# Routing of two experts: a bit search after the loop, or ranks counted in the loop

## The chip, the cores and the metric

One of the eight cores of a Trainium2 chip runs the whole program. The metric is device time in microseconds (us), from the runs and from one profiled execution. PE is TensorE, DVE is VectorE, ACT is ScalarE, POOL is GpSimd, SP is SyncE; each takes its own instructions strictly in the order in which they stand, and waits where the next one isn't ready.

## The reference

One block: a gated linear attention and a Hyena branch, an output projection with a residual, and then a mixture of 16 experts in which every expert chooses its 128 best tokens of 1,024.

```python
def _ec_moe(h, w_router, w_gate, w_up, w_down):
    cap = EC_FACTOR * L // N_EXPERTS            # 128
    aff = jax.nn.softmax((h @ w_router).astype(jnp.float32), axis=-1)
    vals, idx = lax.top_k(jnp.swapaxes(aff, 1, 2), cap)
    xs = h[bidx, idx]
    hid = jax.nn.silu(jnp.einsum('becd,edf->becf', xs, w_gate)) * jnp.einsum('becd,edf->becf', xs, w_up)
    y = jnp.einsum('becf,efd->becd', hid, w_down) * vals[..., None].astype(h.dtype)
    return jnp.zeros_like(h).at[bidx, idx].add(y.astype(h.dtype))
```

## The kernel before, in words

Tokens lie in 8 tiles of 128 (NT). The last loop ahead of the experts runs over the tiles from 7 down to 0, in three steps that are offset by one turn each: `gla_out(i)` makes the attention output, `residual(i)` multiplies by `w_out` (the `pout` matmuls), adds the residual and writes rows to `d_acc` and `d_h`, and `router(i)` computes the affinities of the tile's 128 tokens to the 16 experts: `aff[:, :, i]`, a token on each partition.

After the loop stands the routing. `select(e0, ne, tag, bits)` finds the 128 best tokens for `ne` experts at once by a search over the bits of a float: in each round DVE makes a set of thresholds (`thr`) and compares all affinities with them (`ge`), PE counts over the tokens by 8 matmuls with a matrix of ones (`psel`), and DVE keeps the highest threshold that at least 128 tokens reach (L1283, L1284). A round can't begin before the one ahead is done. `select(0, 2, "a", 5)` serves experts 0 and 1 in 6 rounds of five bits; `select(2, 14, "b", 2)` serves experts 2 to 15 in 15 rounds of two bits. Afterwards `gt`, `eq`, `need`, `keep` and two prefix sums on PE turn the threshold into `pos`, the place of each chosen token from 1 to 128.

`route(e)` compares `pos` with the numbers 1 to 128 (`oh`, L1320, 128x1024 on DVE), gets the token numbers by 8 matmuls (`pi`), writes them to `ix`, and POOL gathers the rows `xs` from `d_h` by an indirect DMA. `transposed` turns them (`ptx`) and splits them in a high and a low part (`thi`, `tlo`).

An expert reads three weights of 8 tiles (128x1024) each: gate, up, down. For a tile ACT makes the high part (`ehi`) and DVE the low part (`elo`), with 5 and 4 buffers, and PE runs 6 matmuls (`pex`, L150 to L152). So a weight is 48 `pex` matmuls. In order of work expert 0 goes gate(0), up(0), gate(1), down(0); inside up(0), after its third tile, the code asks for the transposed rows of expert 1 and for `route(2)`, and inside gate(1) for the transposed product `sg` that down(0) needs. `route(2)` needs all of `select` "b".

The code is written in this order, but a scheduler that lays the program out at build time decides where each instruction stands on its engine, and on the chip that order is fixed. SP issues the weight loads (L1222) into 21 buffers for gate and up and 8 for down, and each load waits for its buffer.

Of the kernel before, what the change touches and what calls it, by code (L numbers as in the profile page):

```python
# [10 lines left out]
F32 = mybir.dt.float32  # L11
F32R = mybir.dt.float32r
BF16 = mybir.dt.bfloat16
I32 = mybir.dt.int32
# [28 lines left out]
def shape_constants():  # L43
    f = np.float32
    out = {}
    quarter = D // 4
    omega = (1.0 / (f(10000.0) ** (np.arange(quarter, dtype=f) / f(quarter)))).astype(f)
    er = (np.arange(16, dtype=f)[:, None] * omega).astype(f)
    ec = (np.arange(64, dtype=f)[:, None] * omega).astype(f)
    out["posr"] = np.concatenate([np.sin(er), np.cos(er)], -1).astype(f)  # L50
    pc = np.concatenate([np.sin(ec), np.cos(ec)], -1).astype(f)
    out["posc"] = np.concatenate([pc, pc], 0)
    out["pos"] = np.concatenate([np.repeat(out["posr"], 64, 0), np.tile(out["posc"], (8, 1))], 1).reshape(8, 128, 1024)
    out["ident"] = np.eye(P, dtype=f)

    n1 = np.arange(8)[None, :, None]
    n2 = np.arange(128)[:, None, None]
    k2 = np.arange(128)[None, None, :]
    th = 2 * np.pi * (k2 + 0.5) * (n1 + 8 * n2) / 2048.0
    fc, fs = np.cos(th), -np.sin(th)  # L60
    out["fmat"] = np.stack([fc, fs], 1).astype(f)
    out["fneg"] = (-fs).astype(f)
    out["imat"] = np.stack([fc.transpose(2, 1, 0) / 1024.0, fs.transpose(2, 1, 0) / 1024.0], 1).astype(f)

    t = np.linspace(0.0, 1.0, L, dtype=f)[:, None]
    w = (f(2.0 * math.pi) * np.arange(L, dtype=f)[:, None] / f(L)).astype(f)
    bands = np.linspace(1e-4, 15, 16, dtype=f)[None, :]
    fw = (bands * w).astype(f)
    z = np.concatenate([t, np.cos(fw), -np.sin(fw)], -1).astype(f)
    n = (np.arange(8)[:, None] + 8 * np.arange(128)[None, :]).reshape(-1)  # L70
    out["zfeat"] = z[n].T.astype(f)
    deltas = np.abs(np.linspace(math.log(1e-2) / 1.5, math.log(1e-2) / 0.3, HYW, dtype=f))
    dec = np.exp(-t * deltas).astype(f)[n].reshape(8, 128, 4, 128)
    out["decay"] = dec.transpose(2, 1, 0, 3).astype(f)

    i16 = 1.0 / 16.0
    tok, col = np.meshgrid(np.arange(P), np.arange(2 * (CH + 2)), indexing="ij")
    pre = (tok // CH == col // (CH + 2)) & (tok % CH < col % (CH + 2))
    out["pre"] = (pre * i16).astype(f)
    ss, cc = np.meshgrid(np.arange(P) % CH, np.arange(CH), indexing="ij")  # L80
    out["smask"] = np.stack([ss <= cc, ss >= cc], 1).astype(np.int32)
    ss, cc = np.meshgrid(np.arange(P), np.arange(P), indexing="ij")
    out["before"] = (ss < cc).astype(f)
    out["slot"] = np.broadcast_to(np.arange(1, P + 1, dtype=f), (P, P)).copy()
    out["sel"] = np.tile(np.eye(32, E, dtype=f), (4, 1))
    tid = np.zeros((P, NT, 2), f)
    tid[:, :, 0] = np.arange(P)[:, None]
    tid[:, :, 1] = P * np.arange(NT)[None, :]
    out["tokid"] = tid
    for b in (5, 2):  # L90
        dig = np.zeros((P, 30 // b, 1 << b), np.int32)
        for i in range(30 // b):
            dig[:, i, :] = np.arange(1 << b) << (30 - b * (i + 1))
        out[f"digit{b}"] = dig
    return {"c_" + k: np.ascontiguousarray(v) for k, v in out.items()}
# [3 lines left out]
def tile_gla_hyena_moe(ctx: ExitStack, tc: tile.TileContext, io: dict, out: bass.AP):  # L99
# [22 lines left out]
    def s2(shape, dt=F32, name="s2"):  # L122
        return s2p.tile(shape, dt, name=name, tag="s2")
# [10 lines left out]
    def cload(name, shape, dt=F32, pool=None, src=None):  # L134
        t = (pool or const).tile(shape, dt, name=name)
        SY.dma_start(t, io["c_" + name] if src is None else src)
        return t
# [807 lines left out]
    def gb(tag, bufs):  # L945
        return lambda shape, name: psg.tile(shape, F32, name=name, tag=tag, bufs=bufs)

    ga, gc, gd, ge1 = gb("ga", 2), gb("gc", 2), gb("gd", 1), gb("ge", 1)

    def chunk_updates(i, e4, vs):  # L950
# [114 lines left out]
    SY.dma_start(slotf, io["c_slot"])  # L1065
    V.tensor_copy(slot, slotf)
    tokid = cload("tokid", [P, NT, 2], pool=keep)
    digit = {b: cload(f"digit{b}", [P, 30 // b, 1 << b], I32, pool=keep) for b in (5, 2)}
    ones = keep.tile([P, P], BF16, name="ones")
    V.memset(ones, 1.0)  # L1070
    before = keep.tile([P, P], BF16, name="before")
    befr = s2([P, P], name="befr")
    SY.dma_start(befr, io["c_before"])
    V.tensor_copy(before, befr)
    ws = [wout_tile(k, op_tile) for k in range(4)]
    p2a.close()
    g2 = p2.enter_context(tc.tile_pool(name="g2", bufs=1, side="right", reuse_waits="tile"))

    def h4(shape, name, tag, bufs, dt=F32):
        return g2.tile(shape, dt, name=name, tag=tag, bufs=bufs)  # L1080


    diag = [g2.tile([P, NH, P], F32, name=f"diag{x}") for x in range(2)]
# [98 lines left out]
        V.reciprocal(sm, sm)  # L1182
        V.tensor_scalar(aff[:, :, i], ex, sm, None, op0=ALU.mult)

    outs, rows = [], []
    for i in reversed(range(-2 - 1, NT)):
        if i >= 0:
            outs.append((i, gla_out(i)))
        if rows:
            router(*rows.pop(0))  # L1190
        if outs and (i < 0 or len(outs) > 1):
            o_ = outs.pop(0)
            rows.append((o_[0], *residual(*o_)))
    p2.close()
    st_stack.close()
    early_stack.close()
# [9 lines left out]
    def pT(shape, name):  # L1206
        return pse.tile(shape, F32, name=name, tag="t", bufs=2)
# [35 lines left out]
    def select(e0, ne, tag, bits):  # L1243

        aff_ = aff[:, e0:e0 + ne]

        def tl(shape, dt, name, bufs=1):
            return mt(shape, dt, name + tag, name + tag, bufs)

        def column_sums(ps, mask):  # L1250
            for t in range(NT):
                T.matmul(ps, ones, mask[:, :, t], start=t == 0, stop=t == NT - 1)  # L1252

        def prefix(ps, mask):
            T.matmul(ps, before, mask, start=True, stop=False)
            for s in range(1, NT):
                T.matmul(ps[:, :, s:], ones, mask[:, :, 0:NT - s], start=False, stop=s == NT - 1)

        if e0 == 0:
            def pr(n):  # L1260
                return pT([P, n], "psel")
        else:
            acc = pse.tile([P, D], F32, name="psel", tag="ex", bufs=3)
            flip = [0]

            def pr(n):
                flip[0] ^= 512
                return acc[:, flip[0]:flip[0] + n]

        base = tl([P, ne], F32, "base")  # L1270
        V.memset(base, 0.0)
        nd = 1 << bits
        for b in range(30 // bits):
            thr = tl([P, nd, ne], F32, "thr", 2)
            V.tensor_tensor(thr.bitcast(I32), digit[bits][:, b, :, None].to_broadcast([P, nd, ne]),
                            base.bitcast(I32)[:, None, :].to_broadcast([P, nd, ne]), op=ALU.bitwise_or)
            ge = tl([P, nd - 1, ne, NT], BF16, "ge")
            V.tensor_tensor(ge, aff_[:, None].to_broadcast([P, nd - 1, ne, NT]),
                            thr[:, 1:nd, :, None].to_broadcast([P, nd - 1, ne, NT]), op=ALU.is_ge)
            pc = pr((nd - 1) * ne)  # L1280
            column_sums(pc, ge.rearrange("p q e t -> p (q e) t"))
            upper = thr[:, 1:nd].rearrange("p q e -> p (q e)")
            V.scalar_tensor_tensor(upper, pc, float(CAP) - 0.5, upper, op0=ALU.is_ge, op1=ALU.mult)  # L1283
            V.tensor_reduce(base, thr.rearrange("p q e -> p e q"), AX.X, ALU.max)  # L1284
        thb = base[:, :, None].to_broadcast([P, ne, NT])
        gt = tl([P, ne, NT], BF16, "gt")
        V.tensor_tensor(gt, aff_, thb, op=ALU.is_gt)
        eq = tl([P, ne, NT], BF16, "eq")
        V.tensor_tensor(eq, aff_, thb, op=ALU.is_equal)
        pg_ = pr(ne)  # L1290
        column_sums(pg_, gt)
        need = tl([P, ne], F32, "need")
        V.tensor_scalar(need, pg_, -1.0, float(CAP), op0=ALU.mult, op1=ALU.add)
        pq_ = pr(ne * NT).rearrange("p (e t) -> p e t", t=NT)
        prefix(pq_, eq)
        keep = tl([P, ne, NT], BF16, "keep")
        V.tensor_tensor(keep, pq_, need[:, :, None].to_broadcast([P, ne, NT]), op=ALU.is_lt)
        V.tensor_mul(keep, keep, eq)
        V.tensor_add(keep, keep, gt)
        pp = pr(ne * NT).rearrange("p (e t) -> p e t", t=NT)  # L1300
        prefix(pp, keep)
        V.scalar_tensor_tensor(pos[:, e0:e0 + ne], pp, 1.0, keep, op0=ALU.add, op1=ALU.mult)

    NF = 2
    select(0, NF, "a", 5)

    tv = mp.tile([P, E, NT, 5], BF16, name="tv")
    V.tensor_copy(tv[:, :, :, 0:2], tokid[:, None].to_broadcast([P, E, NT, 2]))
# [8 lines left out]
    def route(e):  # L1317
        pi = pT([P, 5], "pi")
        oh = mt([P, NT, P], BF16, "oh", "s2", NS)
        V.tensor_tensor(oh, slot[:, None, :].to_broadcast([P, NT, P]),  # L1320
                        pos[:, e, :, None].to_broadcast([P, NT, P]), op=ALU.is_equal)
        for t in range(NT):
            T.matmul(pi, oh[:, t], tv[:, e, t], start=t == 0, stop=t == NT - 1)
        ix = tiny.tile([P, 1], I32, name="ix", bufs=4)
# [121 lines left out]
```

## Time and profile before

| | us |
|---|---|
| median of 3 runs (1383.15 to 1387.09) | 1386.45 |
| the profiled execution, its own time | 1382.24 |
| span of its trace | 1380.5 |

The 1.74 us between span and time lie around the traced program. A position in the trace is given in us from the start of the span. The loop over the tiles ends near 738, the first expert's matmuls begin at 769.62, and the last scatter of an expert's result but one is issued at 1329.29.

### The profile page before, as it was taken

The page shows a single profiled execution, that of the slowest core. Times are in us where ns is not written, and L with a number is a line of the kernel's source. Part 1 is how long each engine was busy: PE and PEld are TensorE (multiplying, and loading weights), DVE is VectorE, ACT ScalarE, POOL GpSimd, SP SyncE. Part 2 cuts the span into 40 slices and gives each one's busy share as a digit, 9 for nine tenths or more (in the row PEclk, how much of TensorE's full clock was granted, in tenths as well). Part 3 has the DMA queues.
Part 4 walks back from the last instruction along what each step waited for, and adds up shares of the span by engine and source line. Part 5 has one row for each costly group of instructions (what it writes and reads, how often), then busy time and mean ns, then how long its engine had stood idle before and what let it go on. Part 6 is the DMA issues. An engine that isn't in the chain of part 4 may idle for free.

```text
span 1380.5 us, 21546 instructions
## 1 busy us (share of the span) xinstructions
PE 1275.1 (92%) x7720; PEld 1043.0 (76%) x7720; DVE 1149.6 (83%) x1920; ACT 806.4 (58%) x1228; POOL 130.1 (9%) x142
## 2 busy tenths in 40 slices
PE   6978999999999997987996899999999999999982
PEld 4777888687898896766775678888888888877762
DVE  6877838899778778878756799999999999988885
ACT  3247453211221415885553578888888888877864
POOL 1110000010100110000000000011111111012010
PEclk9998999999999998998996799999999999999996
DMA  7893541774655536766668689999999999999765
GB/s 223 315 241 118 177 128 47 229 218 146 187 169 167 154 100 186 176 158 174 221 230 348 241 316 357 358 394 381 395 381 390 385 389 383 372 366 370 265 204 223
DMA packets 154362, 354.81 MB, mean 257 GB/s; under 512 B 28389, under 2 KB 74013, under 8 KB 153999
## 3 DMA queue, kind: packets, MB, share of 16 engines
q1 hardware_dynamic: 134911, 292.84, 59.7%
q0 software_dynamic: 19344, 60.61, 15.7%
q8 instruction: 60, 0.98, 0.3%
q14 instruction: 47, 0.39, 0.1%
HBM read 310.89 MB, written 50.89 MB: 262 GB/s over the span
## 4 chain that ended last, share of the span: by engine, by line
PE 45%; DVE 4%; DMA 2%; issue 1%; ACT 1%; SPq 0%; POOLq 0%; POOL 0%; DVEq 0%; ACTq 0%
PE pex L151 13%; PE pex L152 12%; PE pex L150 12%; PE ptx L1341 2%; DVE elo L147 1%; PE psel L1252 1%; PE pout L150 1%; DMA eraw<-w_up 1%; PE pout L151 1%; DVE xf L1414 1%; PE pout L152 1%; DVE state L635 0%; PE po L1123 0%; PE po L1127 0%; DMA xs<-d_h,ix 0%
## 5 line engine op out<-in xcount | busy, mean ns | idle before, releaser
L147 DVE TENSOR_TENSOR elo<-eraw,ehi 128x1024 fp32r<-128x1024 f32 x256 | 302.5, 1219 | 13.0 <-issue 5.9
L151 PE MATMUL pex<-elo,thi 128*128 128x512 f32 x768 | 306.0, 398 | 4.7 <-DVE elo L147 4.4
L150 PE MATMUL pex<-ehi,thi 128*128 128x512 f32 x768 | 305.4, 398 | 2.3 <-ACT thi L144 1.3
L152 PE MATMUL pex<-ehi,tlo 128*128 128x512 f32 x768 | 303.4, 395 | 0.8 <-DVE tlo L147 0.8
L144 ACT ACTIVATE ehi<-eraw 128x1024 fp32r<-128x1024 f32 x256 | 265.0, 1068 | 50.2 <-PE pex L152 49.3
L151 PEld LDWEIGHTS pex<-elo,thi 128*128 128x128 f32 x768 | 145.2, 189 | 40.4 <-DVE elo L147 10.4
L150 PEld LDWEIGHTS pex<-ehi,thi 128*128 128x128 f32 x768 | 145.2, 189 | 34.1 <-ACT thi L144 1.7
L152 PEld LDWEIGHTS pex<-ehi,tlo 128*128 128x128 f32 x768 | 145.0, 189 | 31.7 <-DVE tlo L147 1.2
L147 DVE TENSOR_TENSOR elo<-erawl,ehi 128x1024 fp32r<-128x1024 f32 x128 | 149.4, 1218 | 6.4 <-ACT ehi L144 5.6
L144 ACT ACTIVATE ehi<-erawl 128x1024 fp32r<-128x1024 f32 x128 | 131.3, 1057 | 19.6 <-PE pex L152 18.0
L144 ACT ACTIVATE whi<-wraw 128x1024 fp32r<-128x1024 f32 x30 | 31.8, 1060 | 104.9 <-DMA wraw<-w_in 28.4
L542 PE MATMUL phy<-xh,whi 128*128 128x512 f32 x192 | 77.2, 402 | 11.3 <-ACT whi L144 11.3
L543 PE MATMUL phy<-xl,whi 128*128 128x512 f32 x192 | 76.0, 396 | 0.0
L150 PE MATMUL pvg<-whi,xh 128*128 128x256 f32 x256 | 73.2, 286 | 0.0
L151 PE MATMUL pvg<-wlo,xh 128*128 128x256 f32 x256 | 72.4, 283 | 0.0
L152 PE MATMUL pvg<-whi,xl 128*128 128x256 f32 x256 | 72.4, 283 | 0.0
L1387 POOL DMA_INDIRECT d_acc<-y,ix x15 | 34.6, 2308 | 392.5 <-DVE y L1386 392.5
L1346 ACT ACTIVATE tt<-ptx,fcol,gfcol 128x128 f32<-128x128 f32 x128 | 48.7, 463 | 33.9 <-PE ptx L1341 33.9
L545 PE MATMUL phy<-xh,wlo 128*128 128x512 f32 x192 | 61.9, 399 | 0.0
L438 ACT ACTIVATE D<-pdft 128x512 f32<-128x512 f32 x32 | 19.1, 597 | 68.9 <-PE pdft L468 39.4
L147 DVE TENSOR_TENSOR wlo<-wraw,whi 128x1024 fp32r<-128x1024 f32 x30 | 36.6, 1221 | 21.2 <-ACT whi L144 21.1
L467 PE MATMUL pdft<-kk,fmat 128*128 128x128 f32 x256 | 52.1, 286 | 0.3 <-ACT D L438 0.2
(452 smaller groups left out, 2596.3 us busy)
## 6 DMA issues: line engine op xcount, KB each, us to landing
eraw<-w_gate SPq DMA_DIRECT2D x128, 512.0 KB
eraw<-w_up SPq DMA_DIRECT2D x128, 512.0 KB
erawl<-w_down SPq DMA_DIRECT2D x128, 512.0 KB
wt<-w_ada SPq DMA_DIRECT2D x48, 512.0 KB
wraw<-w_in SPq DMA_DIRECT2D x30, 512.0 KB
kspec<-d_spec SPq DMA_DIRECT2D x16, 512.0 KB
xt<-x SPq DMA_DIRECT2D x8, 512.0 KB
d_spec<-ue POOLq DMA_DIRECT2D x8, 512.0 KB, 5.9
```

The costliest lines, as they stand in the source:

```text
L144: A.activation(hi, src, AF.Copy)
L147: V.tensor_sub(lo, src, hi.bitcast(F32))
L150: T.matmul(out_, lh, rh, start=first, stop=False)
L151: T.matmul(out_, lh, rl, start=False, stop=False)
L152: T.matmul(out_, ll, rh, start=False, stop=last)
L467: T.matmul(ps[:, r], fmat[:, r, m1], kk[m1 // 4][:, 0, m1 % 4], start=True, stop=False)
L542: T.matmul(ps[:, h], hi[:, k], rh[k][:, h], start=k == 0, stop=False)
L543: T.matmul(ps[:, h], hi[:, k], rl[k][:, h], start=False, stop=False)
L545: T.matmul(ps[:, h], lo[:, k], rh[k][:, h], start=False, stop=k == KT - 1)
L1341: T.transpose(pt[:, k], src[:, (4 * g + k) * P:(4 * g + k + 1) * P], ident)
L1346: A.activation(tt[:, k], pt[:, k], AF.Identity, bias=fcol[:, 0, kk_:kk_ + 1], scale=gfcol[:, kk_:kk_ + 1])
L1387: G.indirect_dma_start(out=d_acc[:, :], out_offset=bass.IndirectOffsetOnAxis(ap=ix[:, :1], axis=0), in_=y, in_offset=None, compute_op=ALU.add)
```

## The change

Places for experts 0 and 1 are counted instead of searched. For tile i and expert e the new `rank(i)` lays the tile's 128 affinities along the free dimension, on every partition (a PE transpose of a broadcast, `prow`, copied to `arow` by DVE). It then compares all affinities of tiles i to 7 that are known by now with the tile's own, token by token (`over`, 128 x (8-i)*128, with a count), breaks ties within the tile (`tie`, with a count), and has PE count for each later tile how many of tile i stand above (`pbelow`, one matmul of one column for each later tile). `rk` collects the sums; a rank up to 128 is the place (`pos0`). `rank` is called one turn after its `router`, and for tile 0 right after it; its two PSUM tiles are in the pool that `router` uses too (`gc`). `select` now serves experts 2 to 15 alone, and its PSUM tile always has the tag `ex`.

```diff
+    def rank(i):
+        W = (NT - i) * P
+        for e in range(NF):
+            row = gc([P, P], name="prow")
+            T.transpose(row, aff[:, e, i:i + 1].to_broadcast([P, P]), ident)
+            V.tensor_copy(arow[:, e, i * P:(i + 1) * P], row)
+            a_ = aff[:, e, i:i + 1]
+            over = s2([P, L], BF16, name="over")
+            cnt = tiny.tile([P, 2], F32, name="cnt")
+            V.tensor_scalar(over[:, 0:W], arow[:, e, i * P:], a_, 0.0, op0=ALU.is_gt, op1=ALU.add, accum_out=cnt[:, 0:1])
+            tie = s2([P, P], BF16, name="tie")
+            V.scalar_tensor_tensor(tie, arow[:, e, i * P:(i + 1) * P], a_, after, op0=ALU.is_equal, op1=ALU.mult,
+                                   accum_out=cnt[:, 1:2])
+            V.scalar_tensor_tensor(rk[:, e, i:i + 1], cnt[:, 0:1], cnt[:, 1:2], rk[:, e, i:i + 1], op0=ALU.add, op1=ALU.add)
+            if i + 1 < NT:
+                below = gc([P, NT], name="pbelow")
+                for t in range(i + 1, NT):
+                    T.matmul(below[:, t:t + 1], over[:, (t - i) * P:(t - i + 1) * P], ones[:, 0:1], start=True, stop=True)
+                V.tensor_sub(rk[:, e, i + 1:], rk[:, e, i + 1:], below[:, i + 1:])
+            if i == 0:
+                V.scalar_tensor_tensor(pos0[:, e], rk[:, e], CAP + 0.5, rk[:, e], op0=ALU.is_le, op1=ALU.mult)
+
-    outs, rows = [], []
+    outs, rows, ranks = [], [], []
     for i in reversed(range(-2 - 1, NT)):
         if i >= 0:
             outs.append((i, gla_out(i)))
         if rows:
+            ranks.append(rows[0][0])
             router(*rows.pop(0))
         if outs and (i < 0 or len(outs) > 1):
             o_ = outs.pop(0)
             rows.append((o_[0], *residual(*o_)))
+        while len(ranks) > 1 or ranks == [0]:
+            rank(ranks.pop(0))
...
-    select(0, NF, "a", 5)
...
         V.tensor_tensor(oh, slot[:, None, :].to_broadcast([P, NT, P]),
-                        pos[:, e, :, None].to_broadcast([P, NT, P]), op=ALU.is_equal)
+                        (pos0[:, e] if e < NF else pos[:, e])[:, :, None].to_broadcast([P, NT, P]), op=ALU.is_equal)
```

The order of the instructions changes at three places that the text below speaks of. Line numbers of the changed kernel are higher than those of the kernel before (`elo` is L147 before and L148 now).

First, DVE right after the last affinities, before:

```order
L1183 TENSOR_SCALAR aff<-ex,sm 128x16
L1271 MEMSET basea 128x2
L1308 CAST tv<-tokid 128x128x2
L1275 TENSOR_TENSOR thra<-digit_6045,basea 128x64
L1312 CAST tv<-aff 128x128
L1278 TENSOR_TENSOR gea<-aff,thra 128x496
```

and now (`after` is the mask of later tokens, `pos` with the number 6055 is `pos0`):

```order
L1202 COPY arow<-prow 128x128
L1206 TENSOR_SCALAR over,cnt<-arow,aff 128x1024
L1208 SCALAR_TENSOR_TENSOR tie,cnt<-arow,aff,after 128x128
L1215 TENSOR_TENSOR rk<-rk,pbelow 128x7
L1210 SCALAR_TENSOR_TENSOR rk<-cnt,rk 128x1
L1202 COPY arow<-prow 128x128
L1217 SCALAR_TENSOR_TENSOR pos_6055<-rk 128x8
L1206 TENSOR_SCALAR over,cnt<-arow,aff 128x1024
L1208 SCALAR_TENSOR_TENSOR tie,cnt<-arow,aff,after 128x128
L1215 TENSOR_TENSOR rk<-rk,pbelow 128x7
L1210 SCALAR_TENSOR_TENSOR rk<-cnt,rk 128x1
L1339 CAST tv<-tokid 128x128x2
```

Where the first of six rounds over `gea` began there are now the last ranks of both experts; after two more rows the comparison `oh` of expert 0 follows. The first round of search "b" now stands behind that `oh`, and its first five count matmuls stand on PE ahead of expert 0's `pi`.

Second, PE late in gate(1), before, where `pi` (the last of 8) belongs to `route(2)` and `ptx<-ident,sg` to the rows that down(0) needs:

```order
L1323 MATMUL pi<-tv,oh 128x5
L151 MATMUL pex<-elo,thi 128x512
L152 MATMUL pex<-ehi,tlo 128x512
L1341 MATMUL ptx<-ident,sg 128x128 x4
L150 MATMUL pex<-ehi,thi 128x512
L1341 MATMUL ptx<-ident,sg 128x128 x4
L151 MATMUL pex<-elo,thi 128x512
L152 MATMUL pex<-ehi,tlo 128x512
```

and now, from the last matmuls of `pi` on to the first ones of down(0):

```order
L1354 LDWEIGHTS oh
L1354 MATMUL pi<-tv,oh 128x5
L1372 MATMUL ptx<-ident,sg 128x128 x8
L151 MATMUL pex<-ehi,thi 128x512
L152 MATMUL pex<-elo,thi 128x512
L153 MATMUL pex<-ehi,tlo 128x512
```

Before, the rounds of search "b" and `route(2)` stand between the `pex` matmuls of gate(0), up(0) and gate(1), 2 to 23 `pex` apart. Now 10 of the 15 rounds do; behind the 144th `pex` come 5 rounds in a row (40 `psel` matmuls), then the sums for `gt`, `eq` and `keep`, then `pi` of `route(2)`, then all 8 `ptx<-ident,sg`, and only then the first `pex` of down(0).

Third, DVE at the same place now:

```order
L148 TENSOR_TENSOR elo<-erawl,ehi 128x1024
L1316 SCALAR_TENSOR_TENSOR thrb<-psel,thrb 128x42
L148 TENSOR_TENSOR elo<-erawl,ehi 128x1024
L1317 TENSOR_REDUCE baseb<-thrb 128x14
L148 TENSOR_TENSOR elo<-erawl,ehi 128x1024
L1308 TENSOR_TENSOR thrb<-digit_6045,baseb 128x56
L1311 TENSOR_TENSOR geb<-aff,thrb 128x336
L1316 SCALAR_TENSOR_TENSOR thrb<-psel,thrb 128x42
L1317 TENSOR_REDUCE baseb<-thrb 128x14
L1308 TENSOR_TENSOR thrb<-digit_6045,baseb 128x56
L1311 TENSOR_TENSOR geb<-aff,thrb 128x336
```

From the third of these rounds on nothing but the search stands there: after the fourth `elo` of down(0) come 4 rounds, then `gt`, `eq`, `need`, `keep` (three), `pos`, `oh`, `pv`, `ix`, `iv` and the two `tlo` of `sg`. Before, 7 `elo` stood between `gtb` and those `tlo`.

The other changes of order lie in the last three experts: a pattern in which the transposes of the coming expert's rows stand after 3 or fewer tiles' `ehi` on ACT, instead of 7 or 8, begins with expert 13's rows before and with expert 14's rows now.

## Rows read from the trace of the kernel before

**Rows 1.** The page: busy time of each engine; TensorE's clock in 40 slices.

```profile
PE 1275.1 (92%) x7720; PEld 1043.0 (76%) x7720; DVE 1149.6 (83%) x1920; ACT 806.4 (58%) x1228; POOL 130.1 (9%) x142
...
PEclk9998999999999998998996799999999999999996
```

**Rows 2.** Windows: length, busy of PE, PEld, DVE, ACT, POOL; clock, DMA.

```profile
684.90:695.20 10.30, 10.30 (x84) 7.84 (x82) 5.18 (x21) 6.64 (x24) 0.84 (x2) 1.00 0.63 204
...
737.00:770.00 33.00, 15.85 (x161) 14.09 (x161) 25.20 (x86) 8.02 (x16) 1.79 (x2) 0.50 0.73 287
...
841.00:876.00 35.00, 35.00 (x167) 28.54 (x166) 33.92 (x35) 30.38 (x37) 3.67 (x2) 1.00 0.97 358
```

**Rows 3.** Timeline of DVE, 737 to 760: start, length, instruction.

```profile
737.70 0.29 DVE L1183 TENSOR_SCALAR aff<-ex,sm 128x16 f32<-128x16 f32 x1
...
755.30 0.17 DVE L1287 TENSOR_TENSOR gta<-aff,basea 128x16 bf16<-128x16 f32 x1
...
755.74 0.22 DVE L1275 TENSOR_TENSOR thrb<-digit,baseb 128x56 int32<-128x56 int32 x1
...
757.88 0.22 DVE L1275 TENSOR_TENSOR thrb<-digit,baseb 128x56 int32<-128x56 int32 x1
...
758.01 1.22 DVE L1320 TENSOR_TENSOR oh<-slot,pos 128x1024 bf16<-128x1024 bf16 x1
```

**Rows 4.** Timeline of PE and POOL, 759 to 770.

```profile
759.28 0.37 PE L1323 MATMUL pi<-tv,oh 128*128 128x5 bf16 x8 [1.77 <-DVE oh L1320]
...
760.91 1.25 POOL L1331 DMA_INDIRECT xs<-d_h,ix  x1 [22.91 <-PE psel L1252]
...
766.07 1.94 PE L1341 MATMUL ptx<-ident,xs 128*128 128x128 f32 x8 [5.60 <-DMA xs<-d_h,ix]
...
769.62 0.80 PE L150 MATMUL pex<-ehi,thi 128*128 128x512 f32 x1 [1.02 <-ACT thi L144]
```

**Rows 5.** Timeline of PE, last matmul of the 24th weight tile.

```profile
812.33 0.40 PE L152 MATMUL pex<-ehi,tlo 128*128 128x512 f32 x1
```

**Rows 6.** Chain that ended last, 784 to 792: start, length, instruction.

```profile
784.45 0.23 PE pex L151
...
784.67 0.62 PE psel L1252 x8
...
789.68 0.87 PE ptx L1341 x8
```

**Rows 7.** Groups of DVE: line, instruction, shapes, count; busy, mean ns.

```profile
L1136 DVE SCALAR_TENSOR_TENSOR yg<-po,ors,sgl 128x128 f32<-128x128 f32 x32 | 9.0, 343 | 0.2
...
L1320 DVE TENSOR_TENSOR oh<-slot,pos 128x1024 bf16<-128x1024 bf16 x16 | 19.5, 1218 | 0.0
...
L233 DVE TENSOR_SCALAR sn<-sy 128x512 f32<-128x512 f32 x2 | 0.8, 423 | 0.0
...
L1312 DVE CAST tv<-rest 128x128 bf16<-128x128 f32 x2 | 0.7, 344 | 0.0
```

**Rows 8.** Windows of 4 us: as rows 2, to the DMA rate.

```profile
752.00:756.00 4.00, 2.47 (x37) 2.21 (x35) 3.14 (x16) 0.00 (x0) 0.00 (x0) 0.50 0.41 159
...
772.00:776.00 4.00, 4.00 (x22) 2.99 (x21) 2.78 (x6) 1.83 (x2) 1.44 (x1) 0.85 0.37 101
```

**Rows 9.** Tile xs, the gathered rows: time from issue to landing.

```profile
DMA to landing us min/median/max: 4.6/7.8/12.2
```

**Rows 10.** Waits, 841 to 1159: total us, times, longest.

```profile
ACT ehi L144 <- PE pex L152: 40.2, 130, 0.6
```

**Rows 11.** Timeline of POOL: four of the 15 scatters of expert results.

```profile
897.47 2.31 POOL L1387 DMA_INDIRECT d_acc<-y,ix  x1 [26.36 <-DVE y L1386]
...
1213.99 2.31 POOL L1387 DMA_INDIRECT d_acc<-y,ix  x1 [26.93 <-DVE y L1386]
...
1253.77 2.31 POOL L1387 DMA_INDIRECT d_acc<-y,ix  x1 [32.80 <-DVE y L1386]
...
1329.29 2.29 POOL L1387 DMA_INDIRECT d_acc<-y,ix  x1 [34.88 <-DVE y L1386]
```

More of the change, by code (lines that the diff above doesn't have):

```diff
@@ L83, in shape_constants @@
     out["before"] = (ss < cc).astype(f)
+    out["after"] = (ss > cc).astype(f)
     out["slot"] = np.broadcast_to(np.arange(1, P + 1, dtype=f), (P, P)).copy()
@@ L89, in shape_constants @@
     out["tokid"] = tid
-    for b in (5, 2):
+    for b in (2,):
         dig = np.zeros((P, 30 // b, 1 << b), np.int32)
@@ L946, in gb @@
         return lambda shape, name: psg.tile(shape, F32, name=name, tag=tag, bufs=bufs)
+    NF = 2
     ga, gc, gd, ge1 = gb("ga", 2), gb("gc", 2), gb("gd", 1), gb("ge", 1)
@@ L1067, in tile_gla_hyena_moe @@
     tokid = cload("tokid", [P, NT, 2], pool=keep)
-    digit = {b: cload(f"digit{b}", [P, 30 // b, 1 << b], I32, pool=keep) for b in (5, 2)}
+    digit = {b: cload(f"digit{b}", [P, 30 // b, 1 << b], I32, pool=keep) for b in (2,)}
     ones = keep.tile([P, P], BF16, name="ones")
@@ L1074, in tile_gla_hyena_moe @@
     V.tensor_copy(before, befr)
+    after = keep.tile([P, P], F32, name="after")
+    SY.dma_start(after, io["c_after"])
+    pos0 = keep.tile([P, NF, NT], BF16, name="pos0")
+    rk = keep.tile([P, NF, NT], F32, name="rk")
+    V.tensor_scalar(rk, tokid[:, None, :, 1].to_broadcast([P, NF, NT]), 1.0, None, op0=ALU.add)
     ws = [wout_tile(k, op_tile) for k in range(4)]
@@ L1080, in h4 @@
         return g2.tile(shape, dt, name=name, tag=tag, bufs=bufs)
+    arow = g2.tile([P, NF, L], F32, name="arow")
     diag = [g2.tile([P, NH, P], F32, name=f"diag{x}") for x in range(2)]
@@ L1257, in prefix, with pr @@
                 T.matmul(ps[:, :, s:], ones, mask[:, :, 0:NT - s], start=False, stop=s == NT - 1)
[L1259 to L1268, printed above, removed]
+        acc = pse.tile([P, D], F32, name="psel", tag="ex", bufs=3)
+        flip = [0]
+        def pr(n):
+            flip[0] ^= 512
+            return acc[:, flip[0]:flip[0] + n]
         base = tl([P, ne], F32, "base")
@@ L1302, in select @@
         V.scalar_tensor_tensor(pos[:, e0:e0 + ne], pp, 1.0, keep, op0=ALU.add, op1=ALU.mult)
-    NF = 2
-    select(0, NF, "a", 5)
     tv = mp.tile([P, E, NT, 5], BF16, name="tv")
```

## Prediction

> **What bounds the kernel now.** I read the page first: PE is busy for 92% of the span, and its clock near full but for two slices of .6 and .7 around the end of the tile loop [rows 1]. Then windows, to see whether that holds by stage. One turn of the tile loop is PE's: 10.30 of 10.30 us busy, DVE 5.18 of them (the first row of [rows 2]). The steady experts are PE's too: 35.00 of 35.00 us at clock 1.00, DMA busy .97 of the time but never waited for there, since in 841 to 1159 ACT, which makes the parts of each weight tile, waits 130 times for PE to free a buffer [rows 2, 10]. Between the two lies a stretch that no engine fills: from 737 to 770 PE works 15.85 of 33.00 us at clock .50 [rows 2]. That is a serial chain, which the timelines of DVE, PE and POOL show: last affinities done at 737.99, six rounds, `gta` at 755.30, `oh` at 758.01, `pi` at 759.28, the gather at 760.91, the transposes at 766.07, first `pex` at 769.62 [rows 3, 4]. What shortens this chain is worth its full length, if PE gets no new gap later; what delays PE after 769.62 costs its full length, since PE has no slack to make it good.
>
> **The change, part by part.** The sum is made against the profiled execution, 1382.24 us; the median of the runs shown is 4.2 above it, and I add these at the end.
>
> *Removed.* From the end of `aff` to the start of `oh` the chain took 758.01 - 737.99 = 20.0 us [rows 3]: **-20.0**.
>
> *Added on that path: the last rank.* Both experts' ranks for tile 0 stand on DVE ahead of `oh`: one transpose .24 (1.94 for 8 at half clock [rows 4]); two `arow` copies, two `tie` and two `tv` casts at .34, by the 128x128 row of `yg`; two `over` of 128x1024 at 1.22, by the row of `oh` [rows 7]; and six small operations at .17, by `gta` [rows 3]. That is .24 + 2.04 + 2.44 + 1.02 = 5.7. An `over` from the nearest row of its own kind (`sn`, tensor_scalar with f32 in SBUF, .423 for 512 elements [rows 7]) would be .85, which makes 5.0; four count outputs and three handoffs to PE, for which no row stands here, could make it 7.8 at .3 each. I take **+6.2**.
>
> The Trainium skill, "VectorE: DVE Perf Modes", section "The perf-mode tier table", says that a tensor_scalar on f32 in SBUF runs at twice the rate of a tensor_tensor. The `sn` row agrees; whether an instruction that also writes a count keeps that rate no row shows. By it the two `over` of the last rank and one of tile 1 would cost 1.1 less and the forecast would be 1397.
>
> *Moved ahead of `pi`.* DVE now has `oh` and then the first round of search "b", and five of its count matmuls stand ahead of `pi` on PE. Before, `pi` began .05 after `oh`. I price this with a whole round, 757.88 - 755.74 = 2.14 [rows 3]: **+2.1** (0.5, the handoff alone, to 2.7).
>
> *The gather.* It took 766.07 - 760.91 = 5.2 from its issue; the median of all 16 is 7.8 [rows 4, 9]. Weight loads ran at 287 GB/s in the mean of 737 to 770 and had fallen to 159 by 752 to 756 [rows 2, 8], before the gather; now it goes out about 10 us earlier, among them. Between 0 and 2.7: **+1.5**.
>
> *Rank of tile 1 within the last router's chain.* The router's small product waits on PE behind six count matmuls of that rank, and its logits on DVE stand behind an `over` of 896 elements (1.1). **+1.5** (0 to 3).
>
> *The loop.* In it six ranks of two experts add 12 transposes (.11 each, .87 for 8 [rows 6]) and 30 one-column matmuls (.046 each, .37 for 8 `pi` [rows 4]) to a PE that is full: 2.7. A DVE that is busy for 5.18 of 10.30 takes some 4 us more a turn. **+3.5** with short waits of PE (0, if PE has holes that the window rounds away, to 8).
>
> So the first `pex` moves by -20.0 + 6.2 + 2.1 + 1.5 + 1.5 + 3.5 = **-5.2**, to about 764.4 (-14.5 with all the low ends, +4.2 with all the high ones).
>
> *First `pex` to the 144th.* This took 812.73 - 769.62 = 43.1 [rows 4, 5]. Moved out of it are five rounds' share and the end of the search, moved in are two more rounds: three sums and `pi` (1.8) and eight transposes (.87) less, two times .62 of `psel` more [rows 6]: **-1.4**.
>
> *The new stall.* This is the largest term. `psel` of search "b" now stands 40 times in a row behind the 144th `pex`, with nothing else of PE between, and all later work of PE stands behind `route(2)` and the transposes of `sg`. DVE has four `elo` between the steps of the first of these rounds, and none after. So PE waits for a chain: the first round, with two `elo` of 1.22 [rows 7] ahead of its next thresholds: .62 + .2 + 1.2 + .2 + 1.2 = 3.5. Four rounds at 2.14: 8.6 [rows 3]. From `gt` to `oh` 758.01 - 755.30 = 2.7 for 16 columns [rows 3], taken as 3.3 for the 112 of `gtb`. `oh` 1.22 and `pi` .4: 1.6 [rows 4, 7]. Transposes of `sg` and their high part, 1.7, since `sg` itself is long done (3.55 = 769.62 - 766.07 is what the same step took for expert 0, with copies and an activation between [rows 4]). And the clock: with PE mostly idle it stood at .50 in 737 to 770 [rows 2], and was back at full about 3.6 us after the first `pex`, as the window 772 to 776 at .85 tells [rows 8]; 3.6 us at half speed lose 1.8. Together **+20.5** (17 to 25). Before, these rounds cost almost nothing, since they lay between `pex` matmuls, as the chain from 784.45 to 789.68 shows [rows 6]. PE is the bound for the rest of the experts, so nothing gives this back; buffers fill in the stall, but ACT already waits for PE alone [rows 10].
>
> *The end.* Scatters of experts lie 35.2 apart ((1213.99 - 897.47)/9); the next takes 39.8, the last two 37.8 each [rows 11], since there the coming expert's transposes stand after fewer weight tiles. This pattern now begins one expert later: **-2** (-5 to +3).
>
> Sum: -5.2 - 1.4 + 20.5 - 2 = **+11.9**, to 1394.1 for a profiled execution, 1398 on the median.
>
> **The rivals.** (A) *The stall is made good*: if weights bounded the experts, PE would find full buffers after the stall and catch up. Then -5.2 - 1.4 - 2 = -8.6, 1378 on the median. For it: DMA share .97 [rows 2]. Against it: PE 35.00 of 35.00, and ACT's waits are all for PE [rows 2, 10]. It decides from a late idle time of 10 us or more that the stall can use; the last three periods hold 4.6 + 2 x 2.6 = 9.8 [rows 11]. 7 in 100.
>
> (B) *The front gains more*: the loop takes the ranks for nothing, `over` costs .85 and the gather 5.2, so the first `pex` comes 13 earlier; and the stall is 18. Then -13 - 1.4 + 18 - 2 = +1.6 to +4.4 with 20.5 of stall: 1388 to 1391. For it: DVE's idle half in the loop [rows 2]. Against it: PE has no idle time for 2.7 us of new matmuls. 13 in 100.
>
> (C) *The loop slows*: the ranks' DVE work stands ahead of the chain from `po` through the normalisation to `yg`, for which PE waits, .65 us in each of 14 ranks: +9 in place of 3.5 and 1.5 more for the last turns, which makes +19, 1405. For it: about 100 new small DVE operations; against it: DVE 5.18 of 10.30 [rows 2]. 8 in 100. The Trainium skill, same page, section "The TRN2 errata", says that every operation with a source in SBUF pays a fixed extra time, so that many small ones cost more than their elements. The rows agree: `gta` takes .17 for 16 columns [rows 3].
>
> **How the numbers follow.** The likeliest case, 72 in 100, is +11.9 with 1391 to 1406 for itself. What a measurement can tell from no change is 0.3%, about 4 us. Faster by more than that (below 1382.3) is A with the lowest edge of B, .09. Within 4 us: most of B and the low edge of the likeliest, .13. Slower: .78. The range of 8 in 10 reaches down to B's low end, 1387, and up past C, to 1408, where the stall's 25 would end too (1394.1 + 4.2 + 4.5 = 1403, with 5 more from the front's bounds).
>
> **What the profile after would show.** Right: `oh` of expert 0 about 7 us after the last `aff`, in place of 20; first `pex` about 764; PE idle except for `psel` for some 17 to 20 us between the 144th `pex` and down(0), near 806 to 826, at clock .50, with DVE's `thrb`, `geb`, `baseb` back to back; periods of 35.2 after it. Wrong: a loop turn above 10.8 (C), a first `pex` before 758 (B), periods under 35 after the stall or end periods of 35.2 (A), or a stall under 14 us, if the search were ahead of PE by then and the five rounds had been done while PE still worked on gate(1).

## The result, and the profile after

The changed kernel takes 1402.64 us (median of 4, 1401.16 to 1404.99) against 1386.77 before (4 runs): a ratio of 1.0112, 95% interval 1.0089 to 1.0136. So it is slower by 16 us, inside the forecast's range and 4.6 above its number.

The profiled execution took 1404.99, its span is 1403.1. The page: PE's busy time and clock.

```profile
PE 1280.8 (91%) x7720; PEld 1046.1 (75%) x7720; DVE 1166.8 (83%) x2001; ACT 808.9 (58%) x1228; POOL 126.4 (9%) x142
...
PEclk9998999999999998997996879999999999999996
```

Windows of one loop turn, of the chain ahead of the experts, of the gap ahead of down(0), of what follows it, and of a steady expert (columns as in [rows 2]).

```profile
684.90:695.20 10.30, 10.30 (x87) 7.87 (x79) 6.76 (x34) 6.70 (x23) 1.06 (x2) 1.00 0.67 208
754.00:776.00 22.00, 5.09 (x48) 4.00 (x49) 14.90 (x41) 6.30 (x12) 1.40 (x1) 0.50 0.70 263
817.70:836.10 18.40, 7.28 (x80) 6.17 (x77) 10.89 (x32) 1.65 (x2) 0.46 (x1) 0.56 0.58 198
836.00:840.00 4.00, 4.00 (x11) 3.03 (x10) 2.61 (x3) 2.49 (x4) 0.59 (x1) 0.50 0.42 131
860.00:895.00 35.00, 35.00 (x169) 28.58 (x168) 33.69 (x35) 30.08 (x38) 3.44 (x2) 1.00 1.02 386
```

PE is still full in the loop and in the experts, as in [rows 2]. The chain is 22 us of PE at half clock, busy for 5.09. New is the window 817.7 to 836.1: 18.4 us in which PE is busy for 7.28, and after it 4 us at clock .50.

The chain ahead of the experts, on DVE, then on PE, then on POOL (to be held against [rows 3, 4]).

```profile
753.10 0.24 DVE L1193 TENSOR_SCALAR aff<-ex,sm 128x16 f32<-128x16 f32 x1
...
754.24 1.28 DVE L1206 TENSOR_SCALAR_CACHE_REDUCE over<-arow,aff 128x1024 bf16<-128x1024 f32 x1
...
758.97 1.25 DVE L1351 TENSOR_TENSOR oh<-slot,pos 128x1024 bf16<-128x1024 bf16 x1
...
761.05 0.50 DVE L1311 TENSOR_TENSOR geb<-aff,thrb 128x336 bf16<-128x336 f32 x1
```

```profile
761.97 0.38 PE L1354 MATMUL pi<-tv,oh 128*128 128x5 bf16 x8
...
772.08 1.97 PE L1372 MATMUL ptx<-ident,xs 128*128 128x128 f32 x8 [5.32 <-DMA xs<-d_h,ix]
...
775.66 0.79 PE L151 MATMUL pex<-ehi,thi 128*128 128x512 f32 x1 [1.61 <-ACT thi L145]
```

```profile
763.76 1.40 POOL L1362 DMA_INDIRECT xs<-d_h,ix  x1 [14.60 <-DVE baseb L1317]
```

The last affinities end at 753.34, `oh` begins at 758.97: 5.6 us in place of 20.0. But `aff` itself is 15.3 later, and the first `pex` begins at 775.66, not 769.62. Only two rounds of search "b" begin before the gathered rows are there, with `geb` at 761.05 and 765.43; the third `geb` follows at 777.48, and its count stands on PE behind `ptx` and the first `pex`.

The chain that ended last, at the gap ahead of down(0).

```profile
817.67 0.63 PE psel L1289 x8
818.53 1.13 DVE elo L148
819.81 1.13 DVE elo L148
821.11 0.52 DVE geb L1311
821.67 0.79 PE psel L1289 x8
...
834.13 0.38 PE pi L1354 x8
834.51 1.81 PE ptx L1372 x8
836.32 0.63 PE pex L151
```

The first round of the row waits for two `elo`, then everything is search: `geb`, `psel`, and so on to `pi` at 834.13, the transposes of `sg`, and `pex` at .43 instead of .23 apiece. Before, in [rows 6], a round's count stood among `pex`, and PE did not wait for it. Afterwards ACT's waits are nearly all for PE, as in [rows 10] (three waits for a load make .9 us), and the scatters keep their period (compare [rows 11]).

```profile
ACT ehi L145 <- PE pex L153: 40.6, 129, 1.0
```

```profile
852.13 2.32 POOL L1418 DMA_INDIRECT d_acc<-y,ix  x1 [15.54 <-DVE y L1417]
...
1239.35 2.31 POOL L1418 DMA_INDIRECT d_acc<-y,ix  x1 [25.27 <-DVE y L1417]
...
1351.98 2.28 POOL L1418 DMA_INDIRECT d_acc<-y,ix  x1 [35.19 <-DVE y L1417]
```

**How much of this is the change.** The two profiled spans differ by 22.6 us, the medians by 15.9. In the trace of before the first affinities end at 673.72, in that of after at 678.92, and ahead of them lie only four small set-up instructions of the change. Distances are therefore taken from the end of the first affinities. By them the last scatter comes at 655.6 before and at 673.1 now: **+17.5**, which fits the medians. The first affinities, before and now:

```profile
673.48 0.24 DVE L1183 TENSOR_SCALAR aff<-ex,sm 128x16 f32<-128x16 f32 x1
```

```profile
678.68 0.24 DVE L1193 TENSOR_SCALAR aff<-ex,sm 128x16 f32<-128x16 f32 x1
```

### The profile page after: what moved, and what is told of

It is laid out like the page before. It is cut to its first block, busy times and chain, and to the rows that moved or that the text cites. A ratio compares the mean times of both kernels' runs of the same rounds, so it can differ in the third digit from the quotient of the medians.

```text
span 1403.1 us, 21631 instructions
## 1 busy us (share of the span) xinstructions
PE 1280.8 (91%) x7720; PEld 1046.1 (75%) x7720; DVE 1166.8 (83%) x2001; ACT 808.9 (58%) x1228; POOL 126.4 (9%) x142
## 3 DMA queue, kind: packets, MB, share of 16 engines
q0 software_dynamic: 19344, 60.61, 15.3%
## 4 chain that ended last, share of the span: by engine, by line
PE 46%; DVE 4%; ACT 1%; issue 1%; DMA 1%; POOLq 0%; DVEq 0%; ACTq 0%
PE pex L152 13%; PE pex L153 12%; PE pex L151 12%; PE ptx L1372 2%; PE pout L151 1%; PE pout L152 1%; PE pout L153 1%; DVE elo L148 1%; PE psel L1289 1%; DVE xf L1445 1%; DMA xs<-d_h,ix 1%; DVE over L1206 1%; PE pth L1176 1%; ACT tt L1377 1%; DVE state L636 0%
## 5 line engine op out<-in xcount | busy, mean ns | idle before, releaser
L148 DVE TENSOR_TENSOR elo<-eraw,ehi 128x1024 fp32r<-128x1024 f32 x256 | 303.1, 1221 | 16.6 <-issue 6.9
L148 DVE TENSOR_TENSOR elo<-erawl,ehi 128x1024 fp32r<-128x1024 f32 x128 | 149.8, 1221 | 6.6 <-ACT ehi L145 3.8
L148 DVE TENSOR_TENSOR wlo<-wraw,whi 128x1024 fp32r<-128x1024 f32 x30 | 36.7, 1224 | 23.1 <-ACT whi L145 23.1
```

The costliest lines, as they stand in the source:

```text
L148: V.tensor_sub(lo, src, hi.bitcast(F32))
```

## The experiments

Eleven kernels ran, in three groups, each beside runs of the kernel before. "From the first affinities" means that distance again. Two theories stood at the start. *Cover*: the stall comes from rounds of search "b" that used to run between the rounds of search "a", and the loop's growth from the counting alone. *Others*: the set-up costs 5 us, the ranks make the stall, or the counting is free.

**The changed kernel again.**

> The changed kernel once more. In its first trace the first affinities came 5.2 us later than before (678.9 against 673.7), and no instruction of the change but four small setup ones lies ahead of them. Theory A, that this is the spread from execution to execution: the first affinities end at 673 to 676 here, the time is about 1398 to 1402. Theory B, that the change itself costs 5 us ahead of the loop (one more load, 8 KB of SBUF taken by arow): the first affinities end at 678 to 680 again. Both: PE idle for about 18.5 us but for count matmuls ahead of down(0).

Measured: 1404.94 (1399.19 to 1406.46), ratio 1.0105 (1.007 to 1.0141). The first affinities end at 681.14 and the time is above 1402, neither of which theory A expected. But in the next run, a kernel without any of the change's set-up, they end at 680.88, and in all profiles but that of before between 675.96 and 682.44. So theory A holds and its numbers did not: the profile of before was taken in an early execution. The gap is 18.46, and the last scatter comes 672.3 from the first affinities.

**The kernel before, without the cover.**

```diff
-    select(NF, E - NF, "b", 2)
+    with tc.issue_after(routed[0][3].ins):
+        select(NF, E - NF, "b", 2)
```

> The kernel before, with search b held on DVE until the row numbers of expert 0 are done, so that no round of b lies between the rounds of a. Theory cover: seven rounds of b ran for nothing between those of a, and the stall of the changed kernel comes from their loss, not from the ranks. Then 6 rounds stand in a row ahead of down(0), PE waits there for 20.5 + 2.1 = 22.6 us, the six rounds of a take perhaps 2.5 less, the end 2.7 less: about 1387 + 17 = 1404. Rival, that the ranks or their PSUM tiles make the stall: about 1385 to 1389, since the kernel has no ranks.

Measured: 1405.51 (1403.92 to 1407.6), ratio 1.0123 (1.0092 to 1.0154), on a kernel that searches for experts 0 and 1 and has no ranks. Waits of PE in 817 to 840, and the window of the gap:

```profile
PE psel L1252 <- DVE geb L1278: 8.8, 5, 3.4
```

```profile
818.20:838.80 20.60, 8.12 (x89) 6.82 (x87) 12.09 (x37) 1.66 (x2) 0.51 (x1) 0.59 0.41 133
```

PE waits 8.8 us in five pieces for `geb`, where the changed kernel waits 7.5 in four, and the gap is 20.6 us, 2.1 longer than 18.5: the sixth round. From the last affinities to `oh` it is 17.8, 2.2 less than before, since the rounds of "a" no longer share DVE. The stall is shown to come from the lost cover; the ranks have no part in it.

**The counting alone** (ranks as in the changed kernel, search "a" kept with its digits and PSUM tiles, and its places used).

```diff
+    select(0, NF, "a", 5)
...
-                        (pos0[:, e] if e < NF else pos[:, e])[:, :, None].to_broadcast([P, NT, P]), op=ALU.is_equal)
+                        pos[:, e][:, :, None].to_broadcast([P, NT, P]), op=ALU.is_equal)
```

> Both at once: the ranks are counted as in the changed kernel, but search a is kept and its places are used, so that the price of counting stands alone. Theory: PE's own growth in the loop 3.8, the last router's chain 6.3, the last ranks ahead of the first round of a on DVE about 5: 1387 + 15 = 1402, and no stall ahead of down(0). Rival, that counting is hidden in the loop and only the stall costs: 1387 to 1392. If 5 us more are lost ahead of the loop: 1407.

Measured: 1406.92 (1404.41 to 1408.25), ratio 1.0127 (1.0098 to 1.0157). DVE: the last affinities and `oh`.

```profile
756.61 0.24 DVE L1193 TENSOR_SCALAR aff<-ex,sm 128x16 f32<-128x16 f32 x1
...
782.99 1.22 DVE L1357 TENSOR_TENSOR oh<-slot,pos 128x1024 bf16<-128x1024 bf16 x1
```

There is no gap ahead of down(0). From the first to the last affinities it is 74.4 us, as in the changed kernel, against 64.3 before: counting costs **10.1** in the loop. The last ranks put 6.1 more ahead of `oh`. Counting is not hidden. The time, 1406.92, is that of the case with 5 us lost ahead of the loop, but the trace doesn't show that loss: from the first affinities to the last scatter it is 17.1 longer than before, of the 19.4 in the medians.

**No counting** (places of experts 0 and 1 are the first 128 tokens, so their routing is left out).

```diff
-        while len(ranks) > 1 or ranks == [0]:
-            rank(ranks.pop(0))
...
+    for e in range(NF):
+        V.scalar_tensor_tensor(pos0[:, e], aff[:, e], 0.0, smallpos, op0=ALU.mult, op1=ALU.add)
```

> The changed kernel without the ranks: the places of experts 0 and 1 are a constant (the first 128 tokens) added to zero times the affinities, in one small operation, so that the routing of two experts is left out. Theory: loop as before, chain shorter by 20 - 0.5, pi 1.7 and gather 3.2 later, the stall of 20.5 with its 40 count matmuls still there, first stretch 1.1 and end 2.7 less: 1387 + 2 = 1389. If the changed kernel loses 5 us ahead of the loop by its setup: 1394. If the stall hangs on the ranks: about 1368.

Measured: 1390.34 (1386.57 to 1392.84, 10 runs), ratio 1.0015 (1.0 to 1.003). The first `pex` comes 83.3 from the first affinities, 12.6 earlier than before (95.9), and all of it is lost in a gap of 18.47:

```profile
PE psel L1289 <- DVE geb L1311: 7.5, 4, 3.4
```

The time is near the 1389 expected. So even counting at no price would not have made this kernel faster, in this order of its instructions.

**route(2) asked for later.**

```diff
-            if e + 2 < E:
+            if e + 2 < E and e:
                 routed.append(route(e + 2))
...
+        def hidden():
+            ahead.append(transposed(e, sg))
+            if not e:
+                routed.append(route(e + 2))
...
-            sg_next = gate_part(e + 1, ahead[0], lambda: ahead.append(transposed(e, sg)))
+            sg_next = gate_part(e + 1, ahead[0], hidden)
```

> The changed kernel with route(2) asked for in gate(1) behind the transposes of sg, instead of in up(0), and nothing else. Those transposes and down(0) then no longer stand behind pi of route(2), and the order shows the five rounds spread among the matmuls of down(0) and up(1). Theory: the gap of 18.5 us ahead of down(0) is gone. But the search ends no sooner, and the rows of expert 2 stand right behind its gather: from gt to the first matmul 3.4 + 1.6 + 1.5 + 5 to 8 of gather + 3.6 = 15 to 18 us of waiting there, and the lost clock again. So about 1400 to 1405, the stall only moved. Rival, that weights fill up meanwhile or that the gap was a matter of the one call: 1384 to 1388.

Measured: 1400.78 (1400.57 to 1401.87), ratio 1.0095 (1.0067 to 1.0123). The gap ahead of down(0) is gone, and one of 16.27 stands at 843 to 859, where PE waits for `keep` and then for the gathered rows of expert 2:

```profile
PE ptx L1372 <- DMA xs<-d_h,ix: 5.7, 1, 5.7
PE psel L1292 <- DVE keepb L1332: 3.4, 1, 3.4
```

The stall moved, as forecast: the search ends late, and whoever needs its result waits.

**Three bits a round.**

```diff
-    select(NF, E - NF, "b", 2)
+    select(NF, E - NF, "b", 3)
```

> The changed kernel with three bits a round in search b: 10 rounds with 98 columns in place of 15 with 42. Theory: one round is left behind the 144th matmul in place of five; the stall is that round 2.9, gt to oh 3.4, oh and pi 1.6, transposes 1.7, clock 1.8 = about 11.5 in place of 20.5; the first rounds ahead of the first pex cost about 1 more each. 1403 - 9 + 1 = 1395. Rival, that wider rounds on DVE (geb of 784 elements, about 1 us) cost what the fewer rounds give: 1402 to 1405.

Measured: 1404.38 (1402.77 to 1407.13), ratio 1.0128 (1.0098 to 1.0158): the rival's number, and a miss of the theory. The gap fell from 18.48 to 12.46, by 6.0 where 9 had been worked out. The count matmuls of one round among `pex` in the changed kernel, and in this one, with a wait of PE:

```profile
811.84 0.78 PE L1289 MATMUL psel<-geb,ones 128*128 128x42 bf16 x8
812.40 0.47 PE L153 MATMUL pex<-ehi,tlo 128*128 128x512 f32 x1
```

```profile
793.25 1.56 PE L1289 MATMUL psel<-geb,ones 128*128 128x98 bf16 x8
794.51 0.55 PE L151 MATMUL pex<-ehi,thi 128*128 128x512 f32 x1
...
809.08 0.50 PE L152 MATMUL pex<-elo,thi 128*128 128x512 f32 x1 [1.26 <-DVE elo L148]
```

Among `pex`, where PE is full, eight matmuls of 98 columns take 1.26 of PE from their start to the next `pex`, eight of 42 took .57. Between the first `pex` and the gap the changed kernel has eight such rounds (the first two of its 15 come ahead of the first `pex`) and this kernel seven: 7 x 1.26 - 8 x .57 = 4.3. The one wait for `elo`, 1.26, is new as well. Together that is 5.5, and the stretch takes 47.7 us in place of 42.0.

**Other PSUM tiles for the last ranks.**

```diff
-            row = gc([P, P], name="prow")
+            row = (gc if i > 2 else ga)([P, P], name="prow")
...
-                below = gc([P, NT], name="pbelow")
+                below = (gc if i > 2 else ga)([P, NT], name="pbelow")
```

> The changed kernel with the PSUM tiles of the ranks of tiles 2, 1 and 0 in ga, which nobody uses any more by then, in place of gc, which the router's transposes use. By the order, the transposes of the last router then stand ahead of the counts of tile 2 on PE, and the ranks of tile 1 of expert 1 behind the last affinities. Theory: from the last residual to the last affinities 7.5 to 8 in place of 11.3 us, from there to oh 2.3 more; 1 to 1.5 us in all, about 1402. Rival, that DVE is what holds the chain, not the place in PSUM: 11 us again, 1403 to 1405.

The last residual on DVE, before and in the changed kernel:

```profile
732.35 0.69 DVE L1038 TENSOR_TENSOR xres<-pout,xres 128x512 f32<-128x512 f32 x1 [1.72 <-PE pout L152]
```

```profile
741.36 0.69 DVE L1040 TENSOR_TENSOR xres<-pout,xres 128x512 f32<-128x512 f32 x1
```

PE of the changed kernel at the last router, whose residual is done at 742.05:

```profile
743.43 0.28 PE L1214 MATMUL pbelow<-ones,over 128*128 128x1 bf16 x5 [2.00 <-DVE over L1206]
...
745.41 0.29 PE L1214 MATMUL pbelow<-ones,over 128*128 128x1 bf16 x5 [1.54 <-DVE over L1206]
...
745.57 1.95 PE L1176 MATMUL pth<-ident,xres 128*128 128x128 f32 x8
```

and of this kernel (done at 739.44):

```profile
738.66 0.60 PE L1176 MATMUL pth<-ident,xres 128*128 128x128 f32 x4
...
740.83 0.28 PE L1214 MATMUL pbelow<-ones,over 128*128 128x1 bf16 x5 [0.32 <-DVE over L1206]
```

In the changed kernel the transposes `pth` of the last router stand behind both counts of tile 2, which wait for `over`. With another tag they go first. From the residual to the last affinities it is 6.6 us in place of 11.3 (4.95 before), from there to `oh` 6.8 in place of 5.6. Measured: 1399.44 (1396.9 to 1401.28), ratio 1.0087 (1.0055 to 1.0118), some 3.5 us better by the trace, where 1 to 1.5 had been expected. Nothing but two tags was changed, so the shared tag set that order.

**All three, with a later request.** The edits of the last three runs, and `KU + 3 * (e == 1)` for `KU` in the call of up(e).

> All three: three bits a round, route(2) asked for behind sg, the last ranks in ga; and the rows of expert 2 asked for three weight tiles later in up(1), which gives the gather 28 matmuls, about 7 us. Theory: no gap of more than 3 us is left from the first pex on; what remains against the kernel before are the dearer loop (3.8 + 6.3 - 1.5), the chain without the search, and the end: 1403 - 20.5 + 1 - 1.5 = 1382, which is 5 us under the kernel before. If a wait of 5 us or more comes back at the rows of expert 2: 1387 or more.

Measured: 1404.03 (1402.02 to 1406.51), ratio 1.0125 (1.0096 to 1.0154). A miss: the wide rounds cost what they did, a gap of 7.54 stands at the rows of expert 2, and the period that contains it is 44.0 instead of 35.

**Six rounds in the gather's wait** (with the last ranks in `ga`).

```diff
-    xt = transposed(0, routed[0][2], True)
+    search = select(NF, E - NF, "b", 2)
+    cnt, red = next(search)
+    with tc.issue_after(cnt.ins):
+        xt = transposed(0, routed[0][2], True)
     routed.append(route(1))
-    select(NF, E - NF, "b", 2)
-    with tc.issue_after(routed[0][3].ins):
+    next(search, None)
+    with tc.issue_after(red.ins):
         sg = gate_part(0, xt)
```

Here `select` hands back, after its sixth round, the round's last count matmul and its last DVE instruction, and goes on when called again.

> The kernel with the last ranks in ga, and in addition six rounds of search b ahead of the transposes of expert 0 on PE and ahead of its first elo on DVE, where two stood: PE waits there for the gather anyway. Theory: six rounds of 2.14 from the first geb end about when the gather lands, so the first pex comes at most 1 us later, and two of the five rounds in a row ahead of down(0) are left after the six are done early (the order shows 2 rounds there): the gap falls from 18.5 to about 10, since 3 x 2.14 and part of the first round go. 1399 - 7.5 + 0.5 = 1392. Rival, that the first elo, which now come later, hold PE after the first pex by as much: 1397 to 1400.

Measured: 1395.76 (1391.0 to 1398.56), ratio 1.0049 (1.003 to 1.0068). The gap is 12.06, so three rounds of 2.14 left it; the first `pex` is .8 later. 1392 had been expected. The mechanism holds; the size was off, since the first round of the row and its `elo` stayed, and the last three periods are longer by 1.5 than in the run with the last ranks in `ga`. (The two traces of the changed kernel differ by 1.1 there, so that part may be chance.)

**Six, and route(2) later**, and **seven, and route(2) later** (both with `KU + 3 * (e == 1)`).

> As the run with six rounds in the gather's wait, and route(2) asked for behind the transposes of sg, the rows of expert 2 three weight tiles later in up(1). By the order no round stands beside another one after the first pex, and 22 matmuls (5.2 us) stand between pi of route(2) and the rows it gathers. Theory: no gap ahead of down(0), and 1.5 + 5 to 8 - 5.2 = 1.5 to 4.5 us of waiting at the rows of expert 2: 1399 - 20.5 + 0.5 + 3 + 1 = 1383, below the kernel before. Rival, that PE waits as long in small pieces, for elo on a DVE that has the search to do as well: 1390 to 1395.

> The same with seven rounds ahead of the first transposes. The seventh costs about 2 us ahead of the first pex, and 40 matmuls (9.4 us) stand between pi of route(2) and the rows of expert 2, so that the wait there goes. Theory: 1383 + 2 - 3 = 1382. Rival as in the run with six: 1390 to 1395.

Measured with six: 1393.39 (1389.36 to 1397.21), ratio 1.0042 (1.0021 to 1.0063). 1383 had been expected, so this is a miss. The number is the rival's (1390 to 1395), but not its mechanism: PE does not wait in small pieces. It waits 5.1 for the gathered rows of expert 2, in a gap of 6.74; 1.5 to 4.5 had been expected. The theory also took off the whole gap of the changed kernel, though PE works for 7.28 us of it (much of that at half clock), and that work stays. The gather of those rows was issued at 833.32, right behind the first scatter, and its rows were used at 841.62, after 8.3 us. With seven, where 1382 had been expected: **1386.32** (1382.52 to 1396.38), ratio 1.0002 (.9979 to 1.0025). PE ahead of the first `pex`, and the window in which the changed kernel had its gap:

```profile
768.67 0.78 PE L1289 MATMUL psel<-geb,ones 128*128 128x42 bf16 x8 [1.36 <-DVE geb L1312]
...
769.27 1.92 PE L1375 MATMUL ptx<-ident,xs 128*128 128x128 f32 x8
...
772.79 0.80 PE L151 MATMUL pex<-ehi,thi 128*128 128x512 f32 x1 [1.61 <-ACT thi L145]
```

```profile
805.00:840.00 35.00, 34.90 (x192) 27.36 (x190) 34.52 (x48) 25.54 (x30) 2.82 (x2) 1.00 0.94 315
```

Rounds follow each other at 2.14, seven are done when the transposes begin, and PE is busy for 34.90 of 35.00 us where there were 18.4 of gap. All that the change had lost came back by order alone, to no difference from the kernel before: the first `pex` is at 96.4 from the first affinities, where before had 95.9. None of the eleven beats the kernel before.

## Why the prediction was right, point by point

- *Removed, -20.0, and the last rank, +6.2*: 5.6 us from `aff` to `oh`. Right. An `over` took 1.28, near the bound taken from `oh`, and a count output .08, where the upper bound had .3. The rule of the Trainium skill, "VectorE: DVE Perf Modes", section "The perf-mode tier table", that a tensor_scalar on f32 in SBUF runs at twice the rate of a tensor_tensor, did not hold for `over`, which also counts: the rows at the end show it.
- *`pi`, +2.1*: it begins 3.0 after `oh` in place of 1.27, +1.7. Right.
- *The gather, +1.5 (0 to 2.7)*: 772.08 - 763.76 = 8.3 in place of 5.2, +3.2, above the bound.
- *Rank of tile 1 within the last router's chain, +1.5 (0 to 3)*: **this is the term that was mis-sized.** From the last residual to the last affinities it is 11.3 in place of 4.95, +6.3. The prediction named the count matmuls of one rank ahead of the router's small product, and `over` ahead of its logits. It did not see that the router's first transposes stood behind the counts of tile 2 as well. The run with other PSUM tiles gave back 4.7 of the 6.3 at this place.
- *The loop, +3.5*: from the first affinities to the last residual 63.1 in place of 59.3, +3.8. Right. So the first `pex` moved by +0.8 in place of -5.2: the front, which was to gain, lost.
- *First `pex` to the 144th, -1.4*: 42.0 in place of 43.1, -1.1. Right.
- *The stall, +20.5*: 18.5 of gap, and 10 matmuls at .43 in place of .23 behind it, 2.0: 20.5. Right, and so was the place, 817.7 to 836.1 for "near 806 to 826" (all is later by the terms above and by the earlier execution of before). Two of its pieces were off and cancel in part: the first round took 4.0 for 3.5, the four behind it 7.7 for 8.6. Why rounds were left over the prediction only told as order; the run without the cover shows it: in the kernel before seven `geb` began between 739 and 757, ahead of `oh`, beside the search "a".
- *The end, -2*: from the start of down(0) to the last scatter 515.8 - 2.0 of lost clock in place of 516.6, -2.8. Right.

Together .8 - 1.1 + 20.5 - 2.8 = +17.4, where +11.9 was forecast; the trace has +17.5. Of the 5.5 between them 4.8 are the last router's chain and 1.7 the gather; the other terms give back 1.0.

*The rivals.* (A) fell: nothing of the stall came back, the periods after it are 35.2 and 35.4. (B) fell: the loop did not take the ranks for nothing, counting cost 10.1 there. What B would have made of the time was sound (its upper sum is +4.1, not +4.4): the run without counting had a front gain of 12.6 and took 1390.34, within B's 1388 to 1391. (C) named the size of the loop's loss (+9 and 1.5, where counting cost 10.1), and its 1405 lies nearer to the 1402.64 measured than the forecast's 1398. But its place was wrong: from 684 to 742, where the ranks run, PE waits only once, .4 us, for what is made of `yg`; six tenths of the loss are the last router's chain.

## What to carry to other kernels

A serial search is not only a cost: what runs between its steps is hidden by it. Before taking such a chain away, list what stands between its instructions on each engine, and ask where that work goes. When a static order is laid out at build time, two tags or one call in another place can be worth as much as the change itself, so read the order for what now stands ahead of the instruction that everybody waits for. And a stall that is moved by asking later is not removed: the work that ends late must begin earlier, here in the wait for a gather.

## What the runs showed of the hardware

The comparison with a count, by its longest and shortest form, and the reading of its accumulator:

```profile
L1206 DVE TENSOR_SCALAR_CACHE_REDUCE over<-arow,aff 128x1024 bf16<-128x1024 f32 x2 | 2.6, 1278 | 0.0
...
L1206 DVE DVE_READ_ACCUMULATOR over<-arow,aff 128x1 f32 x16 | 1.3, 83 | 0.0
...
L1206 DVE TENSOR_SCALAR_CACHE_REDUCE over<-arow,aff 128x128 bf16<-128x128 f32 x2 | 0.7, 341 | 0.0
```

From 128 to 1024 elements (f32 in, bf16 out) it grows by .94 us for 896, 1.05 ns an element, while `sn` of the same kind without a count took .423 for 512 [rows 7]. Each count adds .08 on DVE. The output type alone is not the cause: a cast from f32 to bf16 without a count took .212 for 128 elements, where `over` took .341. No run left the count out of `over`, so that the count is the cause is argued.

```profile
L1068 DVE CAST slot<-slotf 128x128 bf16<-128x128 f32 x1 | 0.2, 212 | 0.0
```

The first gather took 8.2 to 8.7 us from issue to use in seven traces (of six kernels) where it went out 7 to 12 us after the last affinities, and 5.2 to 5.8 in the three where it went out 21 to 29 us after them (the kernel before, the one without cover, the one with unused ranks). In [rows 2, 8] weights still fill buffers in that first stretch; that this is the reason is argued, not tried.

Eight count matmuls took .57 of a full PE for 42 columns and 1.26 for 98: 1.5 ns for each further column, where `pex` takes .23 for 512. Their moving operand (the mask, whose columns stream through PE) is read with a stride of 8 elements. In the kernel before, the eight matmuls of a prefix sum over `keep` (112, then 98 down to 14 columns, 504 in all, read in runs of 8 elements down to 1) took .29 to the next `pex`, .58 ns a column:

```profile
804.59 0.22 PE L1255 MATMUL psel<-keepb,before 128*128 128x112 bf16 x1
804.65 0.39 PE L1257 MATMUL psel<-keepb,ones 128*128 128x98 bf16 x7
804.88 0.48 PE L152 MATMUL pex<-ehi,tlo 128*128 128x512 f32 x1
```

That speaks for the stride as the cause; no run changed the stride alone.
